# One-hot matrices of two chunks interleaved as pairs, in place of sixteen chunks interleaved

## The chip, the cores and the metric

The kernel runs on one core of one Trainium2 chip. The time is the device time of that core in microseconds (us). The four runs of the kernel before lie within 0.2% of each other. Each kernel is timed in rounds beside the kernel before on the same chip. A ratio is the mean time of one kernel's fast runs over that of the other's of the same rounds, so it is not quite the ratio of the medians that are quoted.

## The reference

A graph layer: every edge fetches its source node's features, transforms them, and adds the result to its destination node.

```
N, E, D = 4096, 262144, 256
self_out = nodes @ w_self
msg      = nodes[edges_src] @ w_msg
agg      = zeros((N, D)); np.add.at(agg, edges_dst, msg)
return self_out + agg
```

## The kernel before

The kernel never gathers features. VectorE first sorts the edges by destination segment (512 nodes), then source block (128 nodes), then destination. The sorted list is cut into 2048 chunks of 128 edges. For each chunk TensorE counts: a matmul of two one-hot matrices adds the chunk's edges to a table of (source in block) x (destination in segment) in PSUM, the memory to which these matmuls write. One table, a "run", collects about eight chunks. ScalarE copies a finished table to bf16, and four "apply" matmuls multiply it with the transformed features Y of its source block. There are 256 runs, and the time of one is called a period below.

The one-hots are made by VectorE, sixteen chunks at a time, by comparing each edge's value with a constant row (`jrow[p, j, i] = j`). The chunk index `i` is the innermost one:

```python
SL, W, SEGW, RING = 16, 96, 512, 6
def onehots(src, rel, tag):                  # src, rel: [128, 16] bf16
    e = ohp.tile([P, P, SL], BF16, ...)
    tt(out=e[:], in0=src.unsqueeze(1).to_broadcast([P, P, SL]), in1=jrow[:], op=ALU.is_equal)
    d = ohp.tile([P, W, SL], BF16, ...)
    tt(out=d[:], in0=rel.unsqueeze(1).to_broadcast([P, W, SL]), in1=jrow[:, 0:W, :], op=ALU.is_equal)
    return e, d

def count_mm(ap, e, d, ci, start, after=()):
    mm = nc.tensor.matmul(out=ap, lhsT=e[:, :, ci], rhs=d[:, :, ci], start=start, stop=True, ...)
```

So VectorE writes rows of sixteen adjacent values, while TensorE reads one chunk with a step of 16 elements (32 bytes), both for the weights `e` (128 columns) and for the moving operand `d` (96 columns). Where in the table a chunk's 96 columns go depends on the data, so TensorE's own instruction sequencer loads the offsets into registers:

```python
for c in range(NCOL):                        # 2048 chunks
    ...                                      # one-hots every 16 chunks; one "head" matmul per run, fixed address
    if c % 8 == 0:
        regs = [nc.tensor.alloc_register(f"po{c}_{i}") for i in range(8)]
        nc.tensor.load(regs, poffs[0:1, c:c + 8])
    off = nc.tensor.snap(regs[c % 8], donate=True, min_val=0, max_val=RING * SEGW - W)
    count_mm(ring[:, bass.ds(off, W)], e, d, ci, False)
    ...                                      # evacuation by ScalarE; four apply matmuls per run
```

Of the kernel before, what the change touches and what calls it, by code (L numbers as in the profile page):

```python
# [9 lines left out]
P = 128  # L10
FP32 = mybir.dt.float32
BF16 = mybir.dt.bfloat16
I32 = mybir.dt.int32
I64 = mybir.dt.int64

ALU = mybir.AluOpType
# [4 lines left out]
W = 96  # L21
SL = 16
# [18 lines left out]
def kernel(  # L41
# [9 lines left out]
    nc = tc.nc  # L51
# [12 lines left out]
    const = ctx.enter_context(tc.tile_pool(name="const", bufs=1))  # L64
# [25 lines left out]
    for h in range(2):  # L90
# [17 lines left out]
            out=key, in0=dlo, scalar=128.0, in1=slo, op0=ALU.mult, op1=ALU.add  # L108
        )
        nc.vector.scalar_tensor_tensor(  # L110
            out=key, in0=dhi, scalar=float((1 << 21) - (1 << 16)), in1=key,
# [3 lines left out]
            out=key, in0=shi, scalar=float((1 << 16) - P), in1=key,  # L115
# [6 lines left out]
    nc.sync.dma_start(kd[0:1, NCOL:NCOL + 1], ones_sent[:])  # L122
    nc.gpsimd.dma_start(wcat[:, 0:2, :], w_self.rearrange("(k p) f -> p k f", p=P))
    nc.gpsimd.dma_start(wcat[:, 2:4, :], w_msg.rearrange("(k p) f -> p k f", p=P))
    jrow = const.tile([P, P, SL], BF16, name="jrow")
    hbase = const.tile([P, NRUN], FP32, name="hbase")
    thr = const.tile([P, 2], FP32, name="thr")
    lo_c = const.tile([P, G16], I32, name="lo_c")
# [1 line left out]
    lom_c = const.tile([P, G16], I32, name="lom_c")  # L130

    stgn = tc.alloc_tile_pool(name="stage_n", bufs=1)
    jrow_i = stgn.tile([P, P, SL], I32, name="jrow_i")
    nc.gpsimd.iota(jrow_i[:], pattern=[[1, P], [0, SL]], base=0, channel_multiplier=0)
    nc.gpsimd.tensor_copy(out=jrow[:], in_=jrow_i[:])
    hb_i = stgn.tile([P, NRUN], I32, name="hb_i")
    nc.gpsimd.iota(hb_i[:], pattern=[[1, NRUN]], base=0, channel_multiplier=0)
# [2 lines left out]
        out=hbase[:], in0=hbase[:], scalar1=float(SEGW), scalar2=None, op0=ALU.mult  # L140
# [6 lines left out]
        out=thr[:], in0=thr[:], scalar1=float(SEGW), scalar2=-0.5, op0=ALU.mult, op1=ALU.add  # L147
# [11 lines left out]
        pattern=[[0, NPER], [1, RING], [0, 8]], base=0, channel_multiplier=0,  # L159
# [19 lines left out]
    for t in range(T):  # L179
        y_ps = psum_y.tile([P, D], FP32, name="y_ps", tag="y_ps", bufs=2)  # L180
        for k in range(2):
            nc.tensor.matmul(  # L182
                out=y_ps[:], lhsT=XT[:, k, t * P:(t + 1) * P], rhs=wcat[:, 2 + k, :],
                start=(k == 0), stop=(k == 1),
# [30 lines left out]
    tt = nc.vector.tensor_tensor  # L215
# [5 lines left out]
        out=ex[:], in0=dl[:], scalar1=float(W - SEGW), scalar2=0.0, op0=ALU.add, op1=ALU.max  # L221
# [9 lines left out]
        out=wr[:], in0=sl[:], scalar1=float(RING), scalar2=float(-RING * SEGW),  # L231
# [3 lines left out]
        out=wr[:], in0=sl[:], scalar=float(SEGW), in1=wr[:], op0=ALU.mult, op1=ALU.add  # L235
# [20 lines left out]
    for h in range(2):  # L256
        nc.scalar.activation(
            out=junk[:], in_=gball[:], func=ACTF.Sign, bias=thr[:, h:h + 1], scale=-1.0,
# [3 lines left out]
        out=cnt[:], in0=cnt[:], scalar1=0.5, scalar2=float(NCOL // 2 - 1), op0=ALU.mult, op1=ALU.add  # L262
    )
    nc.vector.tensor_scalar(
        out=cidx[:], in0=cnt[:], scalar1=0.0, scalar2=None, op0=ALU.max
# [5 lines left out]
    for h in range(2):  # L271
        xh = meta.tile([P, P], FP32, name=f"xh{h}")
        nc.gpsimd.indirect_dma_start(
            out=xh[:], out_offset=None, in_=xs_dram[:, :],
# [22 lines left out]
    ohp = tc.alloc_tile_pool(name="onehot", bufs=1)  # L297

    def onehots(src, rel, tag):
        e = ohp.tile([P, P, SL], BF16, name="e_oh", tag="e" + tag, bufs=8 if tag == "c" else 2)  # L300
        tt(out=e[:], in0=src.unsqueeze(1).to_broadcast([P, P, SL]), in1=jrow[:], op=ALU.is_equal)  # L301
        d = ohp.tile([P, W, SL], BF16, name="d_oh", tag="d" + tag, bufs=8 if tag == "c" else 2)
        tt(  # L303
            out=d[:], in0=rel.unsqueeze(1).to_broadcast([P, W, SL]), in1=jrow[:, 0:W, :],
            op=ALU.is_equal,
        )
        return e, d

    DEP = mybir.DependencyInfo(mybir.DependencyClass.Sync, mybir.DependencyReason.DATA)
    evac_of = {}  # L310
# [3 lines left out]

    def count_mm(ap, e, d, ci, start, after=()):
        mm = nc.tensor.matmul(  # L316
            out=ap, lhsT=e[:, :, ci], rhs=d[:, :, ci], start=start, stop=True,
            skip_group_check=True,
        ).ins
        tc.declare_no_dep(  # L320
            mm, group="evac", keep=after, reason="disjoint banks by static schedule"
        )
        for i in after:
            tc.add_manual_dep(mm, i.name, DEP, reason="bank free")
        tc.add_to_no_dep_group("count", mm)
        last_mm[0] = mm
        return mm
# [13 lines left out]
    def head_mm(r, he, hd_):  # L341
        b = (r % RING) * SEGW
        after = [evac_of[r - RING]] if r >= RING else []
        count_mm(ring[:, b:b + W], he, hd_, r % SL, True, after)
# [23 lines left out]
    with tc.manual_schedule():  # L368
# [5 lines left out]
        for c in range(NCOL):  # L374
            ci = c % SL
            if ci == 0:
                sl_ = slice(c, c + SL)
                e, d = onehots(slo_b[:, sl_], rel_b[:, sl_], "c")
                r1 = (c + SL + MARG) // 8
                while nhead * SL <= min(r1, NRUN - 1):  # L380
                    hsl_ = slice(nhead * SL, (nhead + 1) * SL)
                    heads[nhead] = onehots(hsl[:, hsl_], hrel[:, hsl_], "h")
                    nhead += 1
            for r in range(NRUN):
                if max(8 * r - MARG, 0) == c:
                    head_mm(r, *heads[r // SL])
# [3 lines that stand above are left out]
            off = nc.tensor.snap(  # L390
                regs[c % 8], donate=True, min_val=0, max_val=RING * SEGW - W
            )
            count_mm(ring[:, bass.ds(off, W)], e, d, ci, False)
            while nev < NRUN and (8 * nev + 7 + MARG <= c or c == NCOL - 1):
                evac(nev)
                todo.append((c + LAG, nev))
                nev += 1
            while todo and (todo[0][0] <= c or c == NCOL - 1):
                apply_run(todo.pop(0)[1])
# [16 lines left out]
        out=hh[:], in0=rho[:], scalar1=float(SEGW), scalar2=float(SEGW), op0=ALU.mult, op1=ALU.add  # L416
    )
    nc.vector.scalar_tensor_tensor(
        out=v[:], in0=gn[:], scalar=1.0, in1=hh[:], op0=ALU.add, op1=ALU.min
# [3 lines left out]
        out=bad[:], in0=v[:], scalar=float(W), in1=bad[:], op0=ALU.is_gt, op1=ALU.add  # L423
# [3 lines left out]
        out=bad[:], in0=v[:], scalar=float(W - 1), in1=bad[:], op0=ALU.is_gt, op1=ALU.add  # L427
# [4 lines left out]
        out=bad[0:1, 0:1], in0=gi[0:1, 0:1], scalar=float(W - 1), in1=bad[0:1, 0:1],  # L432
# [195 lines left out]
```

## Time and profile before

The median is 1193.1 us (1191.9 to 1193.8, 4 runs).

| from the profile of before | |
|---|---|
| sort and preparation | 550.5 us |
| counting and applying (256 periods) | 642.8 us |
| one period, half clock | 2.46 us: 9 counting matmuls 1.63, 4 applies 0.83 |
| one period, full clock | 2.06 us: 9 counting matmuls 1.61, 4 applies 0.45 |
| VectorE one-hot ops | 1224 and 950 ns |

The view of busy time by stretch splits the kernel in two. The columns are the stretch, its length, the busy us (and instructions) of each engine (PE is TensorE's matmuls, PEld its weight loads, DVE VectorE, ACT ScalarE, POOL GpSimd), the mean granted TensorE clock, the DMA share and GB/s:

```profile
core 0: us, PE busy (x) PEld busy (x) DVE busy (x) ACT busy (x) POOL busy (x), PEclk, DMA share, GB/s
0.00:550.50 550.50, 94.77 (x338) 56.32 (x338) 491.56 (x567) 63.52 (x177) 18.10 (x24) 0.68 0.10 24
550.50:1193.30 642.80, 636.18 (x3392) 497.73 (x3392) 294.80 (x285) 158.64 (x272) 0.00 (x0) 0.53 0.02 8
```

VectorE is busy in the first part, TensorE in the second. TensorE is busy 99% of the second part, yet its clock is granted at little over half (0.53). The costliest groups of the page (busy us, mean ns of one, then idle time before them and its releaser):

```profile
L316 PE MATMUL ring<-d_oh,e_oh 128*128 128x96 bf16 x2304 | 460.7, 361 | 5.4 <-DVE d_oh L303 5.0
L301 DVE TENSOR_TENSOR e_oh<-slo_b,jrow 128x2048 bf16<-128x2048 bf16 x128 | 156.7, 1224 | 302.6 <-PE ring L316 302.6
L358 PE MATMUL out_ps<-Y,at 128*128 128x256 bf16 x1024 | 259.2, 407 | 0.0
L303 DVE TENSOR_TENSOR d_oh<-rel_b,jrow 128x1536 bf16<-128x1536 bf16 x128 | 121.6, 950 | 0.0
```

VectorE waits 302.6 us for TensorE to free one-hot buffers; it is not the limit. A matmul is shown as lasting 361 ns, but the next one starts some 180 ns after it, before it has ended. So its cost has to be read from the distance between starts. The timeline of TensorE, first where the clock is half, then where it is full (start, us from the first start to the last end, group):

```profile
583.78 1.81 PE L316 MATMUL ring<-d_oh,e_oh 128*128 128x96 bf16 x9
585.41 1.03 PE L358 MATMUL out_ps<-Y,at 128*128 128x256 bf16 x4
586.24 1.81 PE L316 MATMUL ring<-d_oh,e_oh 128*128 128x96 bf16 x9
```

```profile
800.34 0.62 PE L358 MATMUL out_ps<-Y,at 128*128 128x256 bf16 x4
800.79 1.79 PE L316 MATMUL ring<-d_oh,e_oh 128*128 128x96 bf16 x9
802.40 0.62 PE L358 MATMUL out_ps<-Y,at 128*128 128x256 bf16 x4
```

Nine counting matmuls take 585.41 - 583.78 = 1.63 us at half clock and 802.40 - 800.79 = 1.61 us at full clock. The applies go from 0.83 to 0.45 us. The counting matmuls, though far narrower, do not follow the clock (1.63 against 1.61 us).

### The profile page before, as it was taken

Reading aid. Unit: us, or ns where it says so; the run is one execution under the profiler, and the core shown is the slowest. Engines: PE = TensorE matmul, PEld = TensorE weight load, DVE = VectorE, ACT = ScalarE, POOL = GpSimd, SP = SyncE. Lnnn points to the kernel's source line nnn. Section 1 sums busy time; section 2 is a strip of 40 time slices with the busy share of each in tenths; the row PEclk is TensorE's granted clock in tenths of the full one; section 3 lists DMA queues with packets and bytes.
Section 4 is the critical chain, followed back from the end, with each engine's and each line's share of the span. In section 5 each row is a group of like instructions: output and inputs, shape, how many; then the busy total and the mean of one; then the engine's idle time right before and its main releaser. Section 6 shows DMA issues by size and latency. Waiting matters only on the chain.

```text
span 1193.3 us, 11711 instructions
## 1 busy us (share of the span) xinstructions
PE 731.0 (61%) x3730; PEld 554.1 (46%) x3730; DVE 786.4 (66%) x851; ACT 222.2 (19%) x449; POOL 18.1 (2%) x24
## 2 busy tenths in 40 slices
PE   0133012121211112115999999999999999999997
PEld 0000001010100111004777777777777777777775
DVE  4999998989899999997644553545444444444420
ACT  0011001011101011030222222222222222222222
POOL 5000000000000000000000000000000000000000
PEclk9999995555565555555555555565555555655555
DMA  8411000000000000010000000000000000000000
GB/s 206 99 26 26 4 0 1 0 0 0 0 1 0 0 0 0 0 73 5 1 1 18 1 2 18 1 19 1 1 19 1 5 15 1 19 1 1 19 2 19
DMA packets 25217, 18.03 MB, mean 15 GB/s; under 512 B 11557, under 2 KB 24358, under 8 KB 24390
## 3 DMA queue, kind: packets, MB, share of 16 engines
q1 hardware_dynamic: 19862, 11.59, 3.2%
q0 software_dynamic: 4720, 2.49, 1.6%
q10 hardware_dynamic: 578, 3.16, 0.7%
q8 instruction: 39, 0.64, 0.2%
q14 instruction: 18, 0.15, 0.0%
HBM read 10.12 MB, written 7.37 MB: 15 GB/s over the span
## 4 chain that ended last, share of the span: by engine, by line
PE 58%; DVE 37%; DMA 3%; issue 1%; ACT 0%; DVEq 0%; SPq 0%
PE ring L316 34%; PE out_ps L358 18%; DVE XA_85 L567 6%; DVE XA_84 L567 6%; DVE XA_85 L568 5%; DVE XA_84 L568 5%; DVE XB_86 L567 3%; DVE XB_87 L567 3%; DVE XB_87 L568 3%; DVE XB_86 L568 3%; PE tp_sw L528 3%; DMA XB_86<-in_edges_dst_dram 1%; PE out_ps L353 1%; DMA fd<-bcol 1%; DMA kd<-k_1518 0%
## 5 line engine op out<-in xcount | busy, mean ns | idle before, releaser
L316 PE MATMUL ring<-d_oh,e_oh 128*128 128x96 bf16 x2304 | 460.7, 361 | 5.4 <-DVE d_oh L303 5.0
L316 PEld LDWEIGHTS <-e_oh 128*128 128x128 bf16 x2304 | 348.3, 151 | 87.2 <-issue 6.1
L301 DVE TENSOR_TENSOR e_oh<-slo_b,jrow 128x2048 bf16<-128x2048 bf16 x128 | 156.7, 1224 | 302.6 <-PE ring L316 302.6
L358 PE MATMUL out_ps<-Y,at 128*128 128x256 bf16 x1024 | 259.2, 407 | 0.0
L332 ACT CAST at<-ring 128x512 bf16<-128x512 f32 x256 | 150.0, 586 | 488.6 <-PE ring L316 488.6
L358 PEld LDWEIGHTS <-at 128*128 128x128 bf16 x1024 | 140.1, 137 | 52.9 <-ACT at L332 0.4
L303 DVE TENSOR_TENSOR d_oh<-rel_b,jrow 128x1536 bf16<-128x1536 bf16 x128 | 121.6, 950 | 0.0
L182 PE MATMUL y_ps<-wcat,XT 128*128 128x256 bf16 x64 | 25.2, 394 | 100.0 <-DMA XT<-nodes_bf_dram 100.0
L528 PE MATMUL tp_sw<-ident,XA_84 128*128 128x128 f32 x80 | 20.7, 437 | 88.1 <-DVE XA_84 L568 68.9
L528 PE MATMUL tp_sw<-ident,XA_85 128*128 128x128 f32 x64 | 15.5, 426 | 93.7 <-DVE XA_85 L568 93.7
L567 DVE TENSOR_TENSOR XA_85<-XA_84 128x1024 f32<-128x1024 f32 x56 | 68.6, 1225 | 2.2
L567 DVE TENSOR_TENSOR XA_84<-XA_85 128x1024 f32<-128x1024 f32 x55 | 67.4, 1225 | 2.2
L568 DVE TENSOR_TENSOR XA_85<-XA_84 128x1024 f32<-128x1024 f32 x56 | 68.2, 1218 | 0.0
L568 DVE TENSOR_TENSOR XA_84<-XA_85 128x1024 f32<-128x1024 f32 x55 | 67.0, 1218 | 0.0
L182 PEld LDWEIGHTS <-XT 128*128 128x128 bf16 x64 | 6.6, 104 | 118.3 <-DMA XT<-nodes_bf_dram 118.3
L528 PEld LDWEIGHTS tp_sw<-ident,XA_84 128*128 128x128 f32 x80 | 14.3, 193 | 94.2 <-DVE XA_84 L568 69.9
L528 PEld LDWEIGHTS tp_sw<-ident,XA_85 128*128 128x128 f32 x64 | 11.4, 188 | 97.8 <-DVE XA_85 L568 52.4
L567 DVE TENSOR_TENSOR XB_86<-XB_87 128x1024 f32<-128x1024 f32 x30 | 36.7, 1225 | 1.0
L567 DVE TENSOR_TENSOR XB_87<-XB_86 128x1024 f32<-128x1024 f32 x30 | 36.7, 1225 | 1.0
L519 ACT COPY XB_86<-tp_sw 128x128 f32<-128x128 f32 x40 | 14.9, 376 | 119.2 <-PE tp_sw L528 116.9
L568 DVE TENSOR_TENSOR XB_87<-XB_86 128x1024 f32<-128x1024 f32 x30 | 36.5, 1218 | 0.0
L568 DVE TENSOR_TENSOR XB_86<-XB_87 128x1024 f32<-128x1024 f32 x30 | 36.5, 1217 | 0.0
(478 smaller groups left out, 302.8 us busy)
## 6 DMA issues: line engine op xcount, KB each, us to landing
out_dram<-o_sb SPq DMA_DIRECT2D x16, 256.0 KB, 2.2
XB_86<-in_edges_dst_dram SPq DMA_DIRECT2D x2, 1024.0 KB, 8.5
XB_87<-in_edges_src_dram ACTq DMA_DIRECT2D x2, 1024.0 KB, 8.7
nodes_bf<-in_nodes_dram POOLq DMA_DIRECT2D x1, 2048.0 KB, 18.9
nodes_bf_dram<-nodes_bf SPq DMA_DIRECT2D x1, 2048.0 KB, 8.7
XT<-nodes_bf_dram SPq DMA_TRANSPOSE x64, 2.4
xs_dram<-XA_84 ACTq DMA_DIRECT2D x1, 1024.0 KB
gball<-gd SPq DMA_DIRECT2D x1, 1024.0 KB, 4.6
```

Of the source, the lines that this page charges most:

```text
L182: nc.tensor.matmul(out=y_ps[:], lhsT=XT[:, k, t * P:(t + 1) * P], rhs=wcat[:, 2 + k, :], start=(k == 0), stop=(k == 1),)
L301: tt(out=e[:], in0=src.unsqueeze(1).to_broadcast([P, P, SL]), in1=jrow[:], op=ALU.is_equal)
L303: tt(out=d[:], in0=rel.unsqueeze(1).to_broadcast([P, W, SL]), in1=jrow[:, 0:W, :], op=ALU.is_equal,)
L316: mm = nc.tensor.matmul(out=ap, lhsT=e[:, :, ci], rhs=d[:, :, ci], start=start, stop=True, skip_group_check=True,).ins
L332: ins = nc.scalar.copy(out=at[:], in_=ring[:, b:b + SEGW]).ins
L353: nc.tensor.matmul(out=out_ps[:, t, :], lhsT=XT[:, k, c0:c0 + P], rhs=wcat[:, k, :], start=(k == 0 and t % 2 == 0), stop=False, skip_group ...
L358: nc.tensor.matmul(out=out_ps[:, t, :], lhsT=at[:, t * P:(t + 1) * P], rhs=Y[:, b, :], start=False, stop=(b == T - 1), skip_group_check=True,)
L519: nc.scalar.copy(out=out_ap, in_=in_ap)
L528: nc.tensor.transpose(tp[:], src[:, g * P:(g + 1) * P], ident[:])
L567: nc.vector.tensor_tensor(out=lo_d, in0=lo_s, in1=hi_s, op=ALU.min)
L568: nc.vector.tensor_tensor(out=hi_d, in0=lo_s, in1=hi_s, op=ALU.max)
```

## The change

The intent is to let TensorE read more densely, without giving up what VectorE needs. Chunks are interleaved in pairs. VectorE still writes rows of two adjacent values; TensorE reads with a step of 2 elements (4 bytes). The number of instructions stays the same on every engine.

```diff
-    jrow = const.tile([P, P, SL], BF16, name="jrow")
+    jrow = const.tile([P, P, 2], BF16, name="jrow")
 ...                                          (its iota and copy shrink alike)
     def onehots(src, rel, tag):
-        e = ohp.tile([P, P, SL], BF16, ...)
-        tt(out=e[:], in0=src.unsqueeze(1).to_broadcast([P, P, SL]), in1=jrow[:], op=ALU.is_equal)
-        d = ...
+        res = []
+        for nm, val, wid in (("e", src, P), ("d", rel, W)):
+            o = ohp.tile([P, SL // 2, wid, 2], BF16, ...)
+            shp = [P, SL // 2, wid, 2]
+            tt(out=o[:],
+               in0=val.rearrange("p (g i) -> p g i", i=2).unsqueeze(2).to_broadcast(shp),
+               in1=jrow[:, 0:wid, :].unsqueeze(1).to_broadcast(shp),
+               op=ALU.is_equal)
+            res.append(o)
+        return res
 ...
-            out=ap, lhsT=e[:, :, ci], rhs=d[:, :, ci], ...
+            out=ap, lhsT=e[:, ci // 2, :, ci % 2], rhs=d[:, ci // 2, :, ci % 2], ...
```

More of the change, by code (lines that the diff above doesn't have):

```diff
@@ L132 @@
     stgn = tc.alloc_tile_pool(name="stage_n", bufs=1)
-    jrow_i = stgn.tile([P, P, SL], I32, name="jrow_i")
-    nc.gpsimd.iota(jrow_i[:], pattern=[[1, P], [0, SL]], base=0, channel_multiplier=0)
+    jrow_i = stgn.tile([P, P, 2], I32, name="jrow_i")
+    nc.gpsimd.iota(jrow_i[:], pattern=[[1, P], [0, 2]], base=0, channel_multiplier=0)
     nc.gpsimd.tensor_copy(out=jrow[:], in_=jrow_i[:])
@@ L299, in onehots @@
     def onehots(src, rel, tag):
-        e = ohp.tile([P, P, SL], BF16, name="e_oh", tag="e" + tag, bufs=8 if tag == "c" else 2)
-        tt(out=e[:], in0=src.unsqueeze(1).to_broadcast([P, P, SL]), in1=jrow[:], op=ALU.is_equal)
-        d = ohp.tile([P, W, SL], BF16, name="d_oh", tag="d" + tag, bufs=8 if tag == "c" else 2)
-        tt(
-            out=d[:], in0=rel.unsqueeze(1).to_broadcast([P, W, SL]), in1=jrow[:, 0:W, :],
-            op=ALU.is_equal,
-        )
-        return e, d
+        res = []
+        for nm, val, wid in (("e", src, P), ("d", rel, W)):
+            o = ohp.tile(
+                [P, SL // 2, wid, 2], BF16, name=nm + "_oh", tag=nm + tag,
+                bufs=8 if tag == "c" else 2,
+            )
+            shp = [P, SL // 2, wid, 2]
+            tt(
+                out=o[:],
+                in0=val.rearrange("p (g i) -> p g i", i=2).unsqueeze(2).to_broadcast(shp),
+                in1=jrow[:, 0:wid, :].unsqueeze(1).to_broadcast(shp),
+                op=ALU.is_equal,
+            )
+            res.append(o)
+        return res
     DEP = mybir.DependencyInfo(mybir.DependencyClass.Sync, mybir.DependencyReason.DATA)
@@ L316, in count_mm @@
         mm = nc.tensor.matmul(
-            out=ap, lhsT=e[:, :, ci], rhs=d[:, :, ci], start=start, stop=True,
+            out=ap, lhsT=e[:, ci // 2, :, ci % 2], rhs=d[:, ci // 2, :, ci % 2], start=start, stop=True,
             skip_group_check=True,
```

## The prediction

> **What bounds the kernel.** The windows view splits the 1193 us in two. Up to 550.5 us VectorE sorts (491.6 us busy); the change does not touch that. From 550.5 us to the end (642.8 us) TensorE is busy throughout (636 us), and the chain of waits is TensorE alone: 62.6% counting matmuls (128x96, one-hots), 32.7% apply matmuls (128x256). VectorE, which builds the one-hots, is busy 46% there; its idle time before the "e" matrices (302.6 us, groups view) is waiting for TensorE to free buffers.
>
> **Why counting is slow.** The stage repeats 256 times: 8 chunk matmuls, 1 head matmul, 4 apply matmuls. In the timeline at 576-600 us the period is 2.45 us: 9 counting matmuls take 1.62 us, so 180 ns each, and 4 apply matmuls 0.83 us. At 800-807 us, with the clock granted in full, the applies fall to 0.46 us, but counting stays at 1.60 us, about 178 ns each. So counting is limited by something that does not follow the array clock. The head matmul has a fixed address and the same spacing, so it is not the register address. The first apply after a counting matmul, which has contiguous weights, still starts 175 ns after it; the first counting matmul after an apply starts only 107 ns after it. So the cost belongs to the strided read of the moving operand: 96 elements at about 1.85 ns, each 32 bytes from the last.[...]
>
> **What the change does.** Instruction counts are unchanged on every engine. Matmuls read with step 2. I estimate the spacing of a counting matmul at 80-107 ns (96 to 128 elements at half clock, taking the apply's 213 ns for 256 as scale). VectorE's operands become rows of two with a zero step in the middle, still 16-bit with innermost step 1: I expect them to stay at 1225 and 950 ns[...]; the trace of before has no such shape. Pool's setup copy shrinks by some 3 us, off the path.
>
> **New limit.** At half clock the period becomes 4x213 + 9x107 = 1.82 us (estimate). At full clock it would be about 1.2 us, but the sequencer intervenes: it spends 0.69 us per eight chunks on loading offsets and 0.115 us per register operation before a matmul. Where it was not held back (552-557 us) it needed 1.65-1.69 us per eight chunks, without applies. So the period should lie at 1.67-1.85 us whatever the clock, about 1.75. VectorE needs (2.18 us per sixteen chunks, plus heads) about 1.25 us per period and is no limit; ScalarE 0.59.
>
> **Time.** 256 x (2.44 - 1.75) = 177 us off, all of it on the critical path. 1193.5 - 177 gives 1016 us; range 980 to 1085. Faster by over 2%: 0.94; within 2%: 0.04; slower: 0.02.
>
> **What would show it.** Sort stage still 550 us. Counting matmul spacing at most 110 ns in runs. Gaps before matmuls that follow register operations, at the start of each group of eight after an offset load. VectorE one-hots still about 1225 and 950 ns. Granted clock above 0.53 on average in the stage.
>
> **What would make it wrong.**[...] (b) Step 2 still costs, say 130 ns: about 1065 us. (c) It was weights or a fixed cost between weight load and matmul: little gain. (d) Apply pairs cost sequencer time too: 1.85 us or more, about 1040 us. (e) The clock stays full and applies cost the sequencer nothing: about 990 us.

The trace of before has this read at step 16 alone (175 ns), so that part was the author's estimate. So is the period of "about 1.2 us" at full clock (0.46 us of applies and 9 x 80 ns make 1.18). The "107 ns" from an apply to the next counting matmul are 108 to 110 ns in the trace at full clock.

## The result, and the profile after

The changed kernel takes 989.7 us in the median (988.7 to 990.1, 4 runs), beside 1193.1 us for the kernel before. The ratio is 0.8295 (95% interval 0.828 to 0.831). Run again on another chip, it gave 990.7 us and 0.8293. That lies within the stated range, 26 us under the central figure.

The same view of busy time by stretch:

```profile
0.00:547.50 547.50, 95.14 (x338) 56.36 (x338) 488.93 (x566) 63.74 (x177) 14.26 (x24) 0.74 0.10 24
547.50:988.20 440.70, 322.74 (x3392) 261.58 (x3392) 293.66 (x286) 158.22 (x272) 0.00 (x0) 0.98 0.03 11
```

The sort stage is as it was (in the profiles of all runs, counting starts between 546 and 553 us). The second part went from 642.8 to 440.7 us, which is the whole gain, and TensorE is now busy for 73% of it. The clock is granted in full almost throughout (0.98). The same groups of the page:

```profile
L323 PE MATMUL ring<-d_oh,e_oh 128*128 128x96 bf16 x2304 | 242.3, 206 | 114.9 <-issue 105.0
L307 DVE TENSOR_TENSOR e_oh<-slo_b,jrow 128x2048 bf16<-128x2048 bf16 x128 | 156.5, 1222 | 114.1 <-PE ring L323 114.1
L365 PE MATMUL out_ps<-Y,at 128*128 128x256 bf16 x1024 | 154.3, 273 | 0.2 <-ACT at L339 0.2
L307 DVE TENSOR_TENSOR d_oh<-rel_b,jrow 128x1536 bf16<-128x1536 bf16 x128 | 121.7, 951 | 0.0
```

VectorE's ops take the same time in rows of two as in rows of sixteen (1222 and 951 ns). The counting matmuls now have 114.9 us of idle time before them, and 105.0 of it ended by "issue": the engine waited for nothing that the profile shows, neither data nor another engine. The timeline shows where that idle time sits:

```profile
751.60 0.55 PE L323 MATMUL ring<-d_oh,e_oh 128*128 128x96 bf16 x4 [0.43 <-issue]
751.98 0.60 PE L365 MATMUL out_ps<-Y,at 128*128 128x256 bf16 x4
752.42 0.38 PE L323 MATMUL ring<-d_oh,e_oh 128*128 128x96 bf16 x5
753.23 0.55 PE L323 MATMUL ring<-d_oh,e_oh 128*128 128x96 bf16 x4 [0.43 <-issue]
```

The period is 753.23 - 751.60 = 1.63 us. Once in each there is a gap of 0.43 us. What TensorE's sequencer does then is not in these views, which leave out register instructions, but it is in the records of the trace (start in us, duration, name, operands; weight loads left out). TENSOR_LOAD is the load of eight offsets into registers, FUSED_REGOPS the register operation that forms one matmul's address:

```
  752.339    37 ns  FUSED_REGOPS
  752.419   208 ns  MATMUL        ring<-d_oh,e_oh
  752.454   589 ns  TENSOR_LOAD   <-poffs
  752.464   207 ns  MATMUL        ring<-d_oh,e_oh
  752.508   205 ns  MATMUL        ring<-d_oh,e_oh
  752.552   206 ns  MATMUL        ring<-d_oh,e_oh
  752.595   207 ns  MATMUL        ring<-d_oh,e_oh
  753.144    37 ns  FUSED_REGOPS
  753.229   204 ns  MATMUL        ring<-d_oh,e_oh
  753.259    37 ns  FUSED_REGOPS
```

While the sequencer loads the next eight offsets, TensorE drains what was queued, with 44 ns between starts. Then it stands idle, until the first register operation lets the next matmul go. Over the whole stage the median from the start of a load to the first register operation is 0.691 us, and 0.115 us passes between register operations. 0.691 + 8 x 0.115 = 1.61 us accounts for nearly all of the median period of 1.638 us.

### The profile page after: what moved, and what is told of

The parts are those of the page before. It is cut to its first block, busy times and chain, and to the rows that moved or that the text cites. A ratio compares the mean times of both kernels' runs of the same rounds, so it can differ in the third digit from the quotient of the medians.

```text
span 988.2 us, 11711 instructions
## 1 busy us (share of the span) xinstructions
PE 417.9 (42%) x3730; PEld 317.9 (32%) x3730; DVE 782.6 (79%) x851; ACT 222.0 (22%) x449; POOL 14.3 (1%) x24
## 4 chain that ended last, share of the span: by engine, by line
DVE 49%; PE 35%; issue 12%; DMA 3%; ACT 0%; DVEq 0%; ACTq 0%; SPq 0%
PE ring L323 18%; PE out_ps L365 10%; DVE XA_85 L574 7%; DVE XA_84 L574 7%; DVE XA_85 L575 7%; DVE XA_84 L575 6%; DVE XB_86 L574 4%; DVE XB_87 L574 4%; DVE XB_87 L575 3%; DVE XB_86 L575 3%; PE tp_sw L535 3%; DVE e_oh L307 2%; DVE d_oh L307 2%; DMA XB_86<-in_edges_dst_dram 2%; DMA fd<-bcol 1%
## 5 line engine op out<-in xcount | busy, mean ns | idle before, releaser
L323 PE MATMUL ring<-d_oh,e_oh 128*128 128x96 bf16 x2304 | 242.3, 206 | 114.9 <-issue 105.0
L307 DVE TENSOR_TENSOR e_oh<-slo_b,jrow 128x2048 bf16<-128x2048 bf16 x128 | 156.5, 1222 | 114.1 <-PE ring L323 114.1
L323 PEld LDWEIGHTS <-e_oh 128*128 128x128 bf16 x2304 | 170.2, 98 | 158.9 <-issue 143.5
L365 PE MATMUL out_ps<-Y,at 128*128 128x256 bf16 x1024 | 154.3, 273 | 0.2 <-ACT at L339 0.2
L365 PEld LDWEIGHTS <-at 128*128 128x128 bf16 x1024 | 85.0, 97 | 15.9 <-issue 1.8
L574 DVE TENSOR_TENSOR XA_85<-XA_84 128x1024 f32<-128x1024 f32 x56 | 68.6, 1225 | 2.2
L574 DVE TENSOR_TENSOR XA_84<-XA_85 128x1024 f32<-128x1024 f32 x55 | 67.4, 1225 | 2.2
L574 DVE TENSOR_TENSOR XB_87<-XB_86 128x1024 f32<-128x1024 f32 x30 | 36.8, 1225 | 1.0
L574 DVE TENSOR_TENSOR XB_86<-XB_87 128x1024 f32<-128x1024 f32 x30 | 36.8, 1225 | 1.0
```

Of the source, the lines that this page charges most:

```text
L307: tt(out=o[:], in0=val.rearrange("p (g i) -> p g i", i=2).unsqueeze(2).to_broadcast(shp), in1=jrow[:, 0:wid, :].unsqueeze(1).to_broadcast( ...
L323: mm = nc.tensor.matmul(out=ap, lhsT=e[:, ci // 2, :, ci % 2], rhs=d[:, ci // 2, :, ci % 2], start=start, stop=True, skip_group_check=True ...
L365: nc.tensor.matmul(out=out_ps[:, t, :], lhsT=at[:, t * P:(t + 1) * P], rhs=Y[:, b, :], start=False, stop=(b == T - 1), skip_group_check=True,)
L574: nc.vector.tensor_tensor(out=lo_d, in0=lo_s, in1=hi_s, op=ALU.min)
```

## The experiments

Theory M says that before the change, the strided read of the moving operand `d` bounded counting. Its main rival W says that it was the strided load of the weights `e`. A third view is that register work bounded the kernel before too. Theory S says that after the change the sequencer's register work sets the period. Its rivals are PSUM, evacuation or VectorE.

The main measure is the distance from one matmul's start to the next, worked out from the start times in the trace, over the counting stage where the clock was full. "d alone" goes from the last counting matmul of a group to the first apply after it. The apply's weights are contiguous and its address is fixed, so this distance shows the moving read of `d`. "Pairs" goes from one counting matmul to the next, as the 25th percentile, because in some kernels the larger distances are the sequencer's.

| kernel | step of d | step of e | d alone, ns | pairs, ns | median us |
|---|---|---|---|---|---|
| before | 16 | 16 | 175 | 175 | 1193 to 1198 |
| eights | 8 | 8 | 172 | 176 | 1183.1 |
| e in pairs only | 16 | 2 | 174 | 174 | 1180.7 |
| fours | 4 | 4 | 68 | 90 | 990.6 |
| d in pairs only | 2 | 16 | 44 | 63 | 994.2 |
| the change | 2 | 2 | 43 | 44 | 989.7 |
| ones | 1 | 1 | 42 | 43 | 1114.5 |

### Only d in pairs, only e in pairs

The step of each operand is set by itself (`GE` and `GD` chunks per group):

```diff
-        for nm, val, wid in (("e", src, P), ("d", rel, W)):
+        for nm, val, wid, g in (("e", src, P, GE), ("d", rel, W, GD)):
 ...                                          (2 becomes g in the shapes; one jrow for each g)
-            out=ap, lhsT=e[:, ci // 2, :, ci % 2], rhs=d[:, ci // 2, :, ci % 2], ...
+            out=ap, lhsT=e[:, ci // GE, :, ci % GE], rhs=d[:, ci // GD, :, ci % GD], ...
```

`GE, GD = 16, 2`:

> Only the moving one-hots d are in pairs (step 2); the weights e stay interleaved by sixteen (step 16). Theory M (the strided read of the moving operand was the cost): about 990 us like the full change, counting matmuls under 110 ns apart, because strided weight loads fit within 107 ns and hide. Rival W (the strided weight load was the cost): about 1190 us, spacing 180 ns. If both cost: in between.

`GE, GD = 2, 16`:

> Only the weights e are in pairs; the moving one-hots d stay interleaved by sixteen. Theory M: about 1190 us, spacing still 175 to 180 ns, clock mostly half. Rival W: about 990 us.

With `d` alone in pairs the kernel took 994.2 us, ratio 0.8299 (0.828 to 0.832): the whole gain. With `e` alone it took 1180.7 us, ratio 0.987 (0.984 to 0.990). The lines of the counting matmuls, first `d` alone, then `e` alone:

```profile
L325 PE MATMUL ring<-d_oh,e_oh 128*128 128x96 bf16 x2304 | 261.0, 217 | 96.9 <-issue 86.8
```

```profile
L325 PE MATMUL ring<-d_oh,e_oh 128*128 128x96 bf16 x2304 | 449.8, 355 | 5.6 <-DVE d_oh L309 5.1
```

Theory M stands and W falls. The weights' stride is not quite free. With `d` in pairs, counting matmuls start 63 ns apart instead of 44; that is hidden, because the sequencer issues one only every 115 ns. With `d` at a step of 16, pairs for `e` bring the median distance from 182 to 175 ns, and the kernel gains 1.3%.

### Steps of 4 and of 8

`GE, GD = 4, 4` and `GE, GD = 8, 8` in the same code.

> Both one-hots in groups of four (step 4, 8 bytes apart[...]).[...] the read is still free: about 990 us, spacing near 45 ns in bursts. Rival: the cost grows steadily with the step; then spacing would be about 45 + 2/14 of 135, some 65 ns, hidden too, so the time is 990 us either way and the burst spacing has to tell.

> Both one-hots in groups of eight (step 8, 16 bytes apart[...]).[...] as slow as sixteen, spacing 175 to 180 ns, about 1190 us. Rival (cost grows steadily with the step): spacing about 105 ns, about 1000 to 1060 us.

Before each "Rival" is the theory that the rival stands against: step 4 still free, step 8 as slow as step 16.

Fours took 990.6 us, ratio 0.827, and eights 1183.1 us, ratio 0.988. At step 8 (16 bytes) the moving read alone costs 172 ns, as much as at step 16. At step 4 (8 bytes) it costs 68 ns, and at step 2 43 ns. At step 4 the rival's figure (some 65 ns) came true, and not the 45 ns expected first. But at step 8 the rival expected 105 ns, so growth in step with the distance falls: the jump lies between 8 and 16 bytes. What causes it is not shown. Step 4 is not yet read at full speed (68 ns against 43); step 2 is (43 against 42 at step 1, below). Fours is no faster or slower than the change only because the sequencer, with 115 ns between register operations in the changed kernel, hides 68 and even 90 ns.

### Step 1, the other end

`GE, GD = 1, 1`: TensorE reads contiguously, and VectorE has to repeat each value with an innermost step of 0.

> Groups of one: TensorE reads with step 1, VectorE repeats each of its sixteen values with an innermost step of 0. TensorE spacing in bursts 42 to 44 ns if step 2 was already free, below that if it was not. VectorE:[...] the stage becomes VectorE-bound: about 1140 us.[...]

The expectation had two cases for VectorE: slower on these operands, 1140 us, or at its rate as before, 990 us.

It took 1114.5 us, ratio 0.932. TensorE gains one nanosecond over step 2 (42 against 43), so step 2 was already free. VectorE loses almost half its rate (2274 ns against 1222 in rows of two for `e`, 1742 against 951 for `d`):

```profile
L309 DVE TENSOR_TENSOR e_oh<-slo_b,jrow 128x2048 bf16<-128x2048 bf16 x128 | 291.1, 2274 | 0.0
L309 DVE TENSOR_TENSOR d_oh<-rel_b,jrow 128x1536 bf16<-128x1536 bf16 x128 | 223.0, 1742 | 0.0
```

It has next to no idle time left (busy 549.6 of 554.9 us) and bounds the stage. Of the groups tried, pairs are the smallest that VectorE handles at the rate of sixteen (1222 ns against 1224); why it is slower on groups of one is not shown. My expected 1140 us was 25 us too high, because I summed durations of ops that overlap slightly: some 142 pairs of 2274 and 1742 ns make 570 us (an estimate), more than the 549.6 us that VectorE was busy.

### Fixed addresses, before and after

Both kernels with fixed PSUM addresses in place of register offsets. The result is wrong (relative error 1.29); times and instruction shapes are what counts.

```diff
-            if c % 8 == 0:
-                regs = ...; nc.tensor.load(regs, poffs[0:1, c:c + 8])
-            off = nc.tensor.snap(regs[c % 8], ...)
-            count_mm(ring[:, bass.ds(off, W)], e, d, ci, False)
+            b0 = (c // 8 % RING) * SEGW + min(W * (c % 8 + 1), SEGW - W)
+            count_mm(ring[:, b0:b0 + W], e, d, ci, False)
```

With groups of sixteen, as in the kernel before:

> Kernel before (interleaved by sixteen) with fixed PSUM addresses in place of offsets loaded into registers; the result is wrong on purpose. Theory M (strided read bounds the kernel before): no change, about 1190 us, spacing 175 to 182 ns. Rival (register work bounds it before as well): clearly under 1100 us.

With pairs, as in the changed kernel:

> The changed kernel with fixed PSUM addresses: no offset loads, no register operations; the result is wrong on purpose. Theory S (the sequencer's register work sets the 1.63 us period after the change): the period falls to the next limit, VectorE's one-hots at about 1.24 us, so about 890 us. Rival (something else, such as PSUM or the evacuation latency, sets the period): stays near 990 us.

With sixteen it took 1192.8 us, ratio 0.998 (0.996 to 0.9997), and the counting matmuls' line is as before:

```profile
L325 PE MATMUL ring<-d_oh,e_oh 128*128 128x96 bf16 x2304 | 459.7, 360 | 4.7 <-DVE d_oh L309 4.7
```

So register work cost the kernel before next to nothing. With pairs it took 842.9 us, ratio 0.705. So after the change register work costs about 989.7 - 842.9 = 147 us. With it gone, VectorE is the limit:

```profile
546.00:840.70 294.70, 240.62 (x3392) 216.34 (x3392) 284.40 (x285) 157.02 (x272) 0.00 (x0) 0.97 0.05 16
```

VectorE is busy 284.4 of 294.7 us. That is 1.11 us per period (284.4 / 256), less than the 1.24 us that I expected.

### Offsets loaded once

Fixed addresses remove loads and register operations together. Here only the loads go. The offsets of the first 48 chunks are loaded once and reused (wrong), and each matmul still forms its address from a register. The tables are zeroed first, since reused offsets leave some columns unwritten.

```diff
+    nc.vector.memset(ring[:], 0.0)
 ...
-            if c % 8 == 0:
-                regs = [... for i in range(8)]
-                nc.tensor.load(regs, poffs[0:1, c:c + 8])
+            if c in (0, 24):
+                regs += [... for i in range(24)]
+                nc.tensor.load(regs[c:], poffs[0:1, c:c + 24])
-            off = nc.tensor.snap(regs[c % 8], donate=True, ...)
+            off = nc.tensor.snap(regs[c % 48], donate=c >= NCOL - 48, ...)
```

> The changed kernel, but the offsets are loaded once, for 48 chunks, and reused for all later chunks; each matmul still computes its address from a register. The result is wrong on purpose. Theory S: without the loads the sequencer needs about 8 x 0.115 + 0.04 = 0.96 us per eight chunks, less than VectorE's 1.1 to 1.25 us, so about 845 to 880 us, near the kernel with fixed addresses. Rival (the register operation before each matmul, not the load, sets the period): stays above 950 us.

It took 847.8 us, ratio 0.709, 5 us above the kernel with fixed addresses. Counting starts 4.5 us later here (550.6 against 546.1 us), after the zeroing of the tables. VectorE is again the limit, busy 284.3 of 289.4 us:

```profile
550.60:840.00 289.40, 278.62 (x3392) 245.31 (x3392) 284.30 (x285) 157.33 (x272) 0.00 (x0) 0.98 0.05 15
```

Taking the loads away is enough: eight register operations and their matmuls (8 x 0.115 = 0.92 us) fit under VectorE's 1.11 us. The period of the changed kernel is the sum of both, 0.69 + 0.92 us. Whether taking away the register operations alone would have done as much was not tried.

### Fewer and longer loads

Offsets of 32 and of 16 chunks loaded at once. The results are right.

```diff
-            if c % 8 == 0:
-                regs = [... for i in range(8)]
-                nc.tensor.load(regs, poffs[0:1, c:c + 8])
+            if c % 32 == 0:                  # 16 in the other kernel
+                regs = [... for i in range(32)]
+                nc.tensor.load(regs, poffs[0:1, c:c + 32])
```

> The changed kernel, loading offsets of 32 chunks at once instead of 8; the result is right. Theory S: per eight chunks the load's 0.69 us becomes some 0.2 us if a load costs the same whatever its length, so the sequencer needs about 1.15 us and VectorE's 1.24 us takes over: about 890 to 905 us. If a load's time grows with the number of registers, nearly 990 us.

> Offsets of 16 chunks loaded at once; the result is right. From the loads measured (591 ns for 8 registers, 2131 ns for 32: about 77 ns plus 64 ns a register) the sequencer saves some 90 ns per eight chunks, 0.59 + 0.10 against half of 1.10 + 0.10; with the clock staying full as in the changed kernel, about 23 us less than it: 967 us.[...]

With 32 it took 984.9 us, ratio 0.823. I had hoped for 890 to 905 us; what came true was the other branch of the expectation, a load whose time grows with its registers. A load of 32 registers takes 2131 ns in the median, one of 16 takes 1104, one of 8 takes 591: about 64 ns for each register and only some 77 ns that longer loads can save. With 32 the clock also fell: it was granted in full for 0.78 of the stage, against 0.97 in the changed kernel. The pauses between matmuls are longer (about 2.1 us around a load, against 0.6 us), but that they make the clock fall is not shown: intervals at full clock have them too. Of the 63 intervals between loads, the 31 that ran at full clock took 6.2 us in the median (1.55 per eight chunks), and the 27 with over 30% of their time at half clock took 7.1 us.

With 16 it took 974.7 us, ratio 0.815 (0.814 to 0.816), beside 0.829 for the changed kernel in the same rounds. The clock stayed full (0.97 of the stage). The median interval fell to 3.17 us per sixteen chunks, or 1.58 per eight. This is the fastest right kernel, 1.6% below the change. I expected 967 us. Worked out afterwards from the median intervals of both traces, 256 x (1.638 - 1.584) = 14 us, near the 16 us measured.

## Why the prediction was right

**What bounded the kernel before** was read correctly. The moving operand's strided read set 175 ns per counting matmul, whatever the clock. Neither the weights nor the register address did. The d-only, e-only and fixed-address runs show it.

**VectorE keeps its rate on rows of two**: predicted 1225 and 950 ns, measured 1222 and 951.

**The new limit** was named correctly, with the gap in the right place: after each offset load the matmuls wait for the sequencer. The runs with fixed addresses and with one load show it.

**The size was somewhat off.** I predicted a saving of 256 x 0.69 = 177 us; it was about 203. Three terms were mis-sized, and only the first of them moved the total.
- The period was put at 1.67 to 1.85 us, with 1.75 in the middle. It is 1.638 in the median. The lower end came from 552-557 us of the kernel before, where one of the gaps in each group was 0.155 to 0.26 us instead of 0.115. I took the upper end in case applies cost the sequencer time, or the clock stayed half. Neither happened: the median gap between the register operations on either side of four applies is still 0.115 us. This is case (e) of the prediction, "about 990 us".
- The spacing of a counting matmul was estimated at 80 to 107 ns. It is 43 to 44 at full clock. In the few places where the clock was half it is 80 (median of the half-clock pairs in the run with fixed addresses and pairs). The 107 ns came from counting the 128 columns of the weights at the applies' scale (213 ns for 256 at half clock); pairs of load and matmul 80 ns apart at half clock show that the weight load does not hold a stream of them back that long. That this miss by up to a factor of two hardly moved the total was luck in part: the sequencer's 115 ns hides either figure.
- VectorE's need was put at 1.25 us per period. It is 1.11. This did not matter here, but it sets what can be gained next.

**The rise of the clock** was only predicted as "above 0.53"; it is 0.98. Why it rose is not shown, and the busy share does not tell it: before, TensorE was busy 99% of the stage with the full clock for 5% of it, after the change 73% with the full clock for 97% (clock from the first counting matmul to the last). How much of the gain the rise was worth has no run of its own. It may be much: at full clock the period before was 2.06 us, so against a kernel before at full clock the change would have saved some 256 x (2.06 - 1.64) = 108 us (an estimate). On the other side, at half clock four applies at 213 ns and nine counting matmuls at 80 ns make 1.57 us, just under the sequencer's 1.63 (the two periods wholly at half clock in the run with fixed addresses and pairs took TensorE 1.57 us each). Whether the change would have kept its period at half clock stays open: of its intervals between loads with the usual four applies alone, one ran wholly at half clock. It took 1.91 us, but TensorE was still behind there from eight extra matmuls.

## What to carry to other kernels

When an engine's time does not follow its clock, look at how its operands are laid out: here (1.63 us at half clock, 1.61 at full) the step of one operand alone decided 17% of the kernel, and a layout that suits the writer (sixteen interleaved) can be cut to the smallest group that the writer still handles at the same rate (two: 1222 ns against 1224). Find the next limit in the trace before changing anything. Here it was the sequencer's offset loads, which the views by engine show only as "issue", and which the other layouts that TensorE reads fast did not move: with steps of 4, or with only `d` in pairs, the median interval between loads was 1.64 us as well.
